# Unread transposes at two more places of a one-core trunk layer, and an earlier trace place for the sums of merged tokens

## Chip, cores and metric

The kernel runs on one core of one Trainium2 chip. The metric is device time in microseconds (us), the median of several runs; the kernel before was run three times. One further execution was taken with the profiler, and all rows below come from that one.

## What is computed

One layer of a decoder trunk with four parallel branches, on 256 tokens of width 2048, everything in fp32. The reference, cut to what matters here:

```python
xn = rms_norm(x, ln_g)
(a_q, a_k, a_v, a_g, c_b, c_c, c_h, c_g, s_q, s_k, s_v, s_g, m_q, m_g,
 i_q, i_k, i_w, r_a, r_c, r_s, r_m) = [xn @ w for w in cols]
y_a = moba_attention(a_q, a_k, a_v) * silu(a_g)
y_c = c_b * short_conv(c_c * c_h, conv_w, conv_b) * silu(c_g)
y_s = dsa_attention(s_q, s_k, s_v, i_q, i_k, i_w) * silu(s_g)   # indexer picks the keys
y_m = memory_attention(m_q, mk, mv) * silu(m_g)
merged = (sigmoid(r_a) * (y_a @ w_branch[0]) + sigmoid(r_c) * (y_c @ w_branch[1])
          + sigmoid(r_s) * (y_s @ w_branch[2]) + sigmoid(r_m) * (y_m @ w_branch[3]))
return rms_norm(x + merged @ w_out, final_g)
```

## The kernel before

**Products.** Every fp32 operand is split into a high and a low part of type fp32r, `hi` and `lo` (`split`, L108: a cast on ScalarE, L109, and a subtraction on VectorE, L110), and a product is three matmuls: hi by hi, hi by lo, lo by hi. Where the output is wanted transposed (queries, keys, gates), a block of 256 weight columns is the stationary operand and the 256 tokens are the moving one (`project_t`, `products_t`, L145 to L147): 2 column tiles x 16 chunks x 3 = 96 matmuls of 256 columns a block, four blocks for a section of width 1024. Otherwise the tokens are stationary and the weights move (`project`, `products`, L174 to L176), 512 columns at a time, or 256 in the last two blocks of the output projection. Some 512-column products are done by halves (`by_halves`, a Strassen-like scheme): weight quarters are subtracted from one another on VectorE (`held`, L265, L271, L275, L280) and meet sums of token parts (`sums_of`, L207; `x_sums` for the input, `m_sums` for the merged tokens).

**Weights' way.** SP loads a quarter of 1 MB into one of four slots with tag "raw" (L127 or L197); ScalarE and VectorE split it half by half into rings of four `hi` and `lo` tiles. The tiles `f` and `g` of `sums_of` take slots of the same tag "raw".

**Unread transposes.** `two_transposes` (L149) writes two transposes of the identity into a PSUM bank named `unused` with tag "s" (two banks, shared with the indexer's `lg`, the attention's `s` and the token transposes) that nothing reads. `project_t` calls it ahead of a block when `first` is true: at the first block of each section of queries and keys and at some others (nine pairs in all). `keep_in_program_order` pins each transpose behind the PE instruction traced before it; nothing pins later matmuls behind the transposes.

**Order.** The order of instructions on each engine is not written out by hand: a list scheduler with a timeline model picks, whenever an engine is free, the ready instruction that was traced first. So the place in the trace is a priority. The trace runs: memory branch, indexer (`indexer_parts`, L469; `indexer`, L489, with `lg` matmuls at L495 and L496 and a Relu at L498), sparse queries, keys and values (L637 to L639), sparse attention, the local attention branch, the convolution branch, and the output projection.

**The end.** `finish` (L625) runs, for each half `j` of a branch, the gate columns by halves and then `merge` (L524): the branch product with 512-column matmuls `w`, times the sigmoid, added to `merged`. For the last branch (L687) `parts_of` (L673) transposes merged columns behind each quarter and splits them into `mt`, and `merged_sums` (L684), called between the last gate columns and the last `merge`, allocates `m_sums`. `sums_of` on the first eight chunks of `mt` is traced behind it all, at L688: two additions of 1024 columns (L212), four of 512 (L214 to L217) and four splits. Then `blocks_of` (L704) yields the output projection: 512 columns as block 0, 1024 by halves (with `m_sums`), and blocks 3 and 4 of 256 columns each; every result is added to `x`, squared and scaled (L724 to L742).

Of the kernel before, what the change touches and what calls it, by code (L numbers as in the profile page):

```python
# [28 lines left out]
S_Q, S_K, S_V, S_G = 8 * W, 9 * W, 10 * W, 11 * W  # L29
# [9 lines left out]
FIRST = {}  # L39
# [11 lines left out]
def hybrid_kernel(ctx, tc, x, xT, mem, memT, ln_g, mem_ln_g, w_t, w_n, w_idx, conv_w, conv_b, w_mem_k, w_mem_v,  # L51
# [13 lines left out]
    def bank(name, tag):  # L65

        return banks.tile([P, NB], F32, name=name, tag=tag, bufs=1 if tag in ("pp", "yp") else 2)
# [40 lines left out]
    def split(hi, lo, src):  # L108
        nc.scalar.copy(out=hi, in_=src)  # L109
        nc.vector.tensor_sub(out=lo, in0=src, in1=hi.bitcast(F32))  # L110
# [10 lines left out]
    def split_weights(src, w):  # L121

        c = src.shape[2]
        per, half = 4 * NB // w, 2 * NB // w
        for k0 in range(0, src.shape[1], per):
            raw = raw_tile(w)[:, :, :c]
            nc.sync.dma_start(out=raw, in_=src[:, k0:k0 + per])  # L127
            for h0 in range(0, per, half):
                hi, lo = parts_tiles(w, c, STATIONARY if w == TB else 0)
                split(hi, lo, raw[:, h0:h0 + half])  # L130
                for k in range(half):
                    yield hi[:, k], lo[:, k], k0 + h0 + k
# [9 lines left out]
    def products_t(o, hi, lo, k, nk, act):  # L142

        a = act(k)
        nc.tensor.matmul(o, lhsT=hi, rhs=a[:, 0], start=(k == 0), stop=False)  # L145
        nc.tensor.matmul(o, lhsT=hi, rhs=a[:, 1], start=False, stop=False)  # L146
        nc.tensor.matmul(o, lhsT=lo, rhs=a[:, 0], start=False, stop=(k == nk - 1))  # L147

    def two_transposes():  # L149

        o = bank("unused", "s")
        for i in range(2):
            tc.keep_in_program_order(nc.tensor.transpose(o[:, i * P:(i + 1) * P], ident, ident))

    def project_t(src, act, first=False):

        if first:
            two_transposes()
        nk, c = src.shape[1:]
        tag = next(turn)  # L160
        acc = [bank("acc", tag)[:, :T] for _ in range(0, c, P)]
        for hi, lo, k in split_weights(src, TB):
            for j, c0 in enumerate(range(0, c, P)):
                c1 = min(c0 + P, c)
                products_t(acc[j][:c1 - c0], hi[:, c0:c1], lo[:, c0:c1], k, nk, act)
        return acc

    def copy_t(dst, acc, func=AF.Copy, rows=P):
        for j, a in enumerate(acc):
            nc.scalar.activation(out=dst[:, j], in_=a[:rows], func=func)  # L170
# [7 lines left out]
    def project(src, act, name, t_outer=False):  # L178

        nk, c = src.shape[1:]  # L180
        tag = next(turn)
        acc = [bank(name, tag)[:, :c] for t in range(2)]
        parts = split_weights(src, c)
        if t_outer:
            held = list(parts)
            steps = ((p, t) for t in range(2) for p in held)
        else:
            steps = ((p, t) for p in parts for t in range(2))
        for (hi, lo, k), t in steps:
            a = act(k)[:, :, t * P:(t + 1) * P]  # L190
            products(acc[t], a[:, 0], a[:, 1], hi, lo, k == 0, k == nk - 1)
        return acc
# [14 lines left out]
    def sums_of(act, sums):  # L207

        f = rawp.tile([P, 4 * NB], F32, name="f", tag="raw").rearrange("p (q k t) -> p q k t", q=2, t=T)
        g = rawp.tile([P, 4 * NB], F32, name="g", tag="raw").rearrange("p (s k t) -> p s k t", s=4, t=P)  # L210
        for i in range(2):
            nc.vector.tensor_add(f[:, i], act(4 * i, 4)[:, :, 0].bitcast(F32), act(4 * i, 4)[:, :, 1].bitcast(F32))  # L212
        a11, a21, a12, a22 = (f[:, i, :, t * P:(t + 1) * P] for i in range(2) for t in range(2))
        nc.vector.tensor_add(g[:, 0], a21, a22)  # L214
        nc.vector.tensor_sub(out=g[:, 1], in0=g[:, 0], in1=a11)
        nc.vector.tensor_sub(out=g[:, 2], in0=a11, in1=a21)
        nc.vector.tensor_sub(out=g[:, 3], in0=a12, in1=g[:, 1])  # L217
        for i in range(4):
            split(sums[:, i, :, 0], sums[:, i, :, 1], g[:, i])
# [105 lines left out]
    def nat_tile(name, tag="nat"):  # L325
        return big.tile([P, 2, W], F32, name=name, tag=tag)
# [26 lines left out]
    def to_heads(name, c0):  # L353

        dst = big.tile([P, 8, T], F32, name=name, tag=name)
        for b in range(4):
            copy_t(dst[:, 2 * b:2 * b + 2], project_t(w_t[FIRST[c0] + b], x_act, b == 0))
        return dst

    def to_values(c0, halved):  # L360
# [15 lines left out]
    def to_gate(c0, val):  # L376

        y = y_parts()
        for b in range(4):
            yt = yt_tile()  # L380
            copy_t(yt, project_t(w_t[FIRST[c0] + b], x_act, b == 0 and c0 == C_G), func=AF.Silu)
            gate_parts(y, yt, yt, val, 2 * b)
        return y
# [241 lines left out]
    def finish(b, y, halved=(True, True), after=None, last=None):  # L625

        for j in range(2):
            sig = gate_columns(b, j, halved[j])
            if j == 1 and last is not None:
                last()  # L630
            merge(b, j, sig, y, after)
# [3 lines left out]

    mask_s = indexer(*indexer_parts())
    q = to_heads("qt", S_Q)  # L637
    k = to_heads("kt", S_K)
    v = to_values(S_V, True)  # L639
    masked_attention(q, k, v, mask_s)  # L640
    finish(BR_S, to_gate(S_G, q))


    q = to_heads("qt", A_Q)
    k = to_heads("kt", A_K)
    v = to_values(A_V, True)
# [24 lines left out]
    mt = big.tile([P, KC, 2, T], F32R, name="mt", tag="xhl")  # L671
# [10 lines left out]
    m_sums = []  # L682

    def merged_sums():  # L684
        m_sums.append(big.tile([P, 4, 4, 2, P], F32R, name="m_sums", tag="m16b"))

    finish(BR_C, to_gate(C_G, cc), after=parts_of, last=merged_sums)  # L687
    sums_of(lambda k0, n: mt[:, k0:k0 + n], m_sums[0])  # L688


    xr = [big.tile([P, D], F32, name=f"xr{t}", tag=tag) for t, tag in ((0, "qt"), (1, "kt"))]
# [12 lines left out]
    def blocks_of():  # L704

        def block(n):
            c0, c = blocks[n]
            acc = project(w_out[c0 // NB][:, :, c0 % NB:c0 % NB + c], lambda k: mt[:, k], "o", t_outer=(n == last))
            return ((n, t, acc[t]) for t in range(2))

        yield from block(0)
        got = []
        nat = nat_tile("no")
        by_halves([w_out[1], w_out[2]], lambda k: mt[:, k], m_sums[0], nat,
                  lambda t, n, src, psum: got.append((1 + n, t, src)), ("y",))
        yield from got
        for n in range(3, last + 1):
            yield from block(n)

    for n, t, src in blocks_of():  # L720
        c0, c = blocks[n]
# [60 lines left out]
```

## Time and profile before

| what | value |
|---|---|
| runs of the kernel | 1362.73, 1363.07, 1364.81 us, median 1363.07 |
| the profiled execution, its own time | 1364.0 us |
| its span, first to last instruction | 1362.2 us |
| TensorE matmuls | 1352.2 us busy (99%), 8386 instructions |
| VectorE | 1007.4 us busy (74%) |
| ScalarE | 786.6 us busy (58%) |
| GpSimd | 11.2 us busy (1%) |
| bytes read from HBM | 265.88 MB, 197 GB/s over the span |

How to read it: an engine's busy time is the union of its records. Matmuls are pipelined, so their records overlap, and the distance between two starts says more than a duration. "PE" is TensorE's matmuls, "PEld" its weight loads, DVE VectorE, ACT ScalarE, SP the engine that issues the loads. Times of rows count from the start of the span.

### The profile page before, as it was taken

The numbers are of one execution on the slowest core, as the hardware profiler recorded it, in microseconds if no ns is written. First come the engines' busy times: TensorE is split into PE (matmuls) and PEld (weight loads), VectorE is DVE, ScalarE is ACT, GpSimd is POOL, SyncE is SP. The second block draws the span as 40 slices with busy tenths as digits, with TensorE's granted clock in tenths as the row PEclk, the third lists the DMA queues.
The fourth block names the chain that finished last, engine by engine and source line by source line (L and its number), as shares of the span: only waits on it lengthen the run. The fifth ranks groups of instructions, "written<-read, shape, count | busy, mean of one in ns | idle before, by whom it ended". The sixth has DMA issues, their size and how long they took to land.

```text
span 1362.2 us, 20606 instructions
## 1 busy us (share of the span) xinstructions
PE 1352.2 (99%) x8386; PEld 1214.2 (89%) x8386; DVE 1007.4 (74%) x1171; ACT 786.6 (58%) x1066; POOL 11.2 (1%) x26
## 2 busy tenths in 40 slices
PE   9999999999999999999999999999999999999997
PEld 9998998889999899888999899888888999888877
DVE  7687665784756878787545878887888758798786
ACT  7663665463445677646444678646455445656553
POOL 1000000000000000000000000000000000000000
PEclk9999999999999999999999999999999999999999
DMA  9864545655556454656555555566565556655752
GB/s 346 302 254 175 200 155 178 216 175 178 193 186 216 160 172 165 210 191 215 187 189 197 180 178 176 171 218 208 185 210 198 192 200 222 207 180 203 249 182 92
DMA packets 49966, 269.43 MB, mean 198 GB/s; under 512 B 6656, under 2 KB 17456, under 8 KB 19024
## 3 DMA queue, kind: packets, MB, share of 16 engines
q1 hardware_dynamic: 48960, 264.03, 56.1%
q0 software_dynamic: 624, 3.31, 0.7%
q8 instruction: 65, 1.06, 0.3%
q10 hardware_dynamic: 288, 0.79, 0.1%
q14 instruction: 29, 0.24, 0.0%
HBM read 265.88 MB, written 2.10 MB: 197 GB/s over the span
## 4 chain that ended last, share of the span: by engine, by line
PE 95%; DVE 2%; ACT 1%; DMA 1%; issue 1%; SPq 0%; POOLq 0%; POOL 0%; DVEq 0%; ACTq 0%
PE acc L145 12%; PE acc L146 11%; PE acc L147 11%; PE w L174 4%; PE w L176 4%; PE w L175 4%; PE u L174 4%; PE u L175 4%; PE u L176 4%; PE m L174 3%; PE m L175 3%; PE m L176 3%; PE y L175 2%; PE y L176 2%; PE x L175 2%; PE x L176 2%
## 5 line engine op out<-in xcount | busy, mean ns | idle before, releaser
L110 DVE TENSOR_TENSOR lo<-raw,hi 128x1024 fp32r<-128x1024 f32 (+1 forms) x472 | 561.5, 1199 | 296.9 <-ACT hi L109 293.1
L109 ACT CAST hi<-raw 128x1024 fp32r<-128x1024 f32 (+1 forms) x472 | 485.0, 1031 | 426.8 <-PE acc L146 149.0
L145 PE MATMUL acc<-x_hl,hi 128*128 128x256 f32 x1264 | 353.7, 280 | 0.0
L146 PE MATMUL acc<-x_hl,hi 128*128 128x256 f32 x1264 | 351.7, 278 | 0.0
L147 PE MATMUL acc<-x_hl,lo 128*128 128x256 f32 x1264 | 351.5, 278 | 0.0
L147 PEld LDWEIGHTS acc<-x_hl,lo 128*128 128x128 f32 x1264 | 237.2, 188 | 0.1
L145 PEld LDWEIGHTS acc<-x_hl,hi 128*128 128x128 f32 x1264 | 237.0, 187 | 0.1
L146 PEld LDWEIGHTS acc<-x_hl,hi 128*128 128x128 f32 x1264 | 237.0, 187 | 0.1
L110 DVE TENSOR_TENSOR lo<-held,hi 128x1024 fp32r<-128x1024 f32 x96 | 115.1, 1221 | 13.6 <-ACT hi L109 13.3
L109 ACT CAST hi<-held 128x1024 fp32r<-128x1024 f32 x96 | 100.2, 1054 | 13.4 <-PE u L176 4.6
L176 PE MATMUL w<-hi,y 128*128 128x512 f32 x256 | 99.7, 389 | 0.0
L175 PE MATMUL w<-lo,y 128*128 128x512 f32 x256 | 99.7, 389 | 0.0
L174 PE MATMUL w<-hi,y 128*128 128x512 f32 x256 | 98.6, 390 | 0.0
L176 PEld LDWEIGHTS w<-hi,y 128*128 128x128 f32 x256 | 48.1, 188 | 10.0
L175 PEld LDWEIGHTS w<-lo,y 128*128 128x128 f32 x256 | 48.1, 188 | 9.9
L174 PEld LDWEIGHTS w<-hi,y 128*128 128x128 f32 x256 | 48.0, 188 | 9.9
L174 PE MATMUL y<-hi,x_hl 128*128 128x512 f32 x132 | 51.7, 392 | 0.0
L176 PE MATMUL u<-hi,x_hl 128*128 128x512 f32 x132 | 51.6, 391 | 0.0
L175 PE MATMUL u<-lo,x_hl 128*128 128x512 f32 x132 | 51.4, 390 | 0.0
L174 PE MATMUL u<-hi,x_hl 128*128 128x512 f32 x132 | 51.4, 390 | 0.0
L176 PE MATMUL y<-hi,x_hl 128*128 128x512 f32 x132 | 51.4, 389 | 0.0
L175 PE MATMUL y<-lo,x_hl 128*128 128x512 f32 x132 | 51.4, 389 | 0.0
(317 smaller groups left out, 2363.6 us busy)
## 6 DMA issues: line engine op xcount, KB each, us to landing
raw<-in_w_n SPq DMA_DIRECT2D x96, 1024.0 KB, 4.9
raw<-in_w_t SPq DMA_DIRECT2D x76, 1024.0 KB, 5.0
raw<-in_w_branch SPq DMA_DIRECT2D x32, 1024.0 KB, 5.0
raw<-in_w_out SPq DMA_DIRECT2D x16, 1024.0 KB, 4.8
raw<-in_w_mem_k SPq DMA_DIRECT2D x8, 1024.0 KB, 5.5
raw<-in_w_mem_v SPq DMA_DIRECT2D x8, 1024.0 KB, 4.9
raw<-in_w_t SPq DMA_DIRECT2D x16, 256.0 KB, 5.8
raw<-in_memT SPq DMA_DIRECT2D x2, 1024.0 KB, 8.2
```

The costliest lines, as they stand in the source:

```text
L109: nc.scalar.copy(out=hi, in_=src)
L110: nc.vector.tensor_sub(out=lo, in0=src, in1=hi.bitcast(F32))
L145: nc.tensor.matmul(o, lhsT=hi, rhs=a[:, 0], start=(k == 0), stop=False)
L146: nc.tensor.matmul(o, lhsT=hi, rhs=a[:, 1], start=False, stop=False)
L147: nc.tensor.matmul(o, lhsT=lo, rhs=a[:, 0], start=False, stop=(k == nk - 1))
L174: nc.tensor.matmul(o, lhsT=ah, rhs=hi, start=start, stop=False, **kw)
L175: nc.tensor.matmul(o, lhsT=ah, rhs=lo, start=False, stop=False, **kw)
L176: nc.tensor.matmul(o, lhsT=al, rhs=hi, start=False, stop=stop, **kw)
```

## The change

Three edits. In `to_heads` the block with `b == 1` of the sparse queries gets a pair of unread transposes too. `sums_of` on the merged tokens is traced inside `merged_sums`, so ahead of the last branch's second `merge`, and no longer behind it. In `blocks_of` a pair of unread transposes is traced between the halved part and the last two blocks of 256 columns.

```diff
@@ -354,7 +354,7 @@
 
         dst = big.tile([P, 8, T], F32, name=name, tag=name)
         for b in range(4):
-            copy_t(dst[:, 2 * b:2 * b + 2], project_t(w_t[FIRST[c0] + b], x_act, b == 0))
+            copy_t(dst[:, 2 * b:2 * b + 2], project_t(w_t[FIRST[c0] + b], x_act, b == 0 or c0 == S_Q and b == 1))
         return dst
 
     def to_values(c0, halved):
@@ -683,9 +683,9 @@
 
     def merged_sums():
         m_sums.append(big.tile([P, 4, 4, 2, P], F32R, name="m_sums", tag="m16b"))
+        sums_of(lambda k0, n: mt[:, k0:k0 + n], m_sums[0])
 
     finish(BR_C, to_gate(C_G, cc), after=parts_of, last=merged_sums)
-    sums_of(lambda k0, n: mt[:, k0:k0 + n], m_sums[0])
 
 
     xr = [big.tile([P, D], F32, name=f"xr{t}", tag=tag) for t, tag in ((0, "qt"), (1, "kt"))]
@@ -714,6 +714,7 @@
         by_halves([w_out[1], w_out[2]], lambda k: mt[:, k], m_sums[0], nat,
                   lambda t, n, src, psum: got.append((1 + n, t, src)), ("y",))
         yield from got
+        two_transposes()
         for n in range(3, last + 1):
             yield from block(n)
 
```

## Rows read from the trace of the kernel before

**Rows 1.** The page: TensorE's granted clock by slice; the chain's shares by engine.
```profile
PEclk9999999999999999999999999999999999999999
...
PE 95%; DVE 2%; ACT 1%; DMA 1%; issue 1%; SPq 0%; POOLq 0%; POOL 0%; DVEq 0%; ACTq 0%
```

**Rows 2.** Timeline of PE, sparse queries and keys: start us, us, engine, line, operation.
```profile
355.63 0.28 PE L145 MATMUL acc<-x_hl,hi 128*128 128x256 f32 x1
...
389.20 0.38 PE L153 MATMUL unused<-ident 128*128 128x128 f32 x2
...
389.53 0.28 PE L146 MATMUL acc<-x_hl,hi 128*128 128x256 f32 x1
...
432.95 0.40 PE L174 MATMUL u<-hi,x_hl 128*128 128x512 f32 x1
```

**Rows 3.** Timeline of PE: first and last of the output's 256-column matmuls.
```profile
1331.96 0.28 PE L174 MATMUL o<-hi,mt 128*128 128x256 f32 x1
...
1354.46 0.28 PE L176 MATMUL o<-hi,mt 128*128 128x256 f32 x1
```

**Rows 4.** Timeline of PE at a pair behind 512-column products; the transposes' group.
```profile
656.50 0.38 PE L153 MATMUL unused<-ident 128*128 128x128 f32 x2
...
656.84 0.28 PE L146 MATMUL acc<-x_hl,hi 128*128 128x256 f32 x1
...
700.26 0.38 PE L153 MATMUL unused<-ident 128*128 128x128 f32 x2
...
L153 PE MATMUL unused<-ident x18: 270/271/273, 28.6 to 1095.9; 128*128 128x128 f32 x18
```

**Rows 5.** Timelines of PE and ACT where the sparse queries' second block begins.
```profile
354.61 0.60 PE L496 MATMUL lg<-it 128*128 128x256 f32 x2
354.86 0.47 PE L145 MATMUL acc<-x_hl,hi 128*128 128x256 f32 x1
...
355.29 0.38 PE L153 MATMUL unused<-ident 128*128 128x128 f32 x2
...
355.43 0.49 ACT L498 ACTIVATE sm<-lg 128x384 f32<-128x384 f32 x1
```

**Rows 6.** Timeline of PE at eight token transposes in the convolution branch.
```profile
1061.22 1.04 PE L350 MATMUL tp<-ident,uu 128*128 128x128 f32 x8
...
1062.22 0.28 PE L146 MATMUL acc<-x_hl,hi 128*128 128x256 f32 x1
...
1064.57 0.28 PE L145 MATMUL acc<-x_hl,hi 128*128 128x256 f32 x1
```

**Rows 7.** The sums' additions and splits, and their first reader (ns min/median/max, first to last start).
```profile
L212 DVE TENSOR_TENSOR f<-mt x2: 1219/1220/1220, 1248.1 to 1255.3; 128x1024 f32<-128x1024 f32 x2
...
L174 PEld LDWEIGHTS m<-hi,m_sums x5: 188/188/188, 1298.0 to 1308.7; 128*128 128x128 f32 x5
...
L110 DVE TENSOR_TENSOR m_sums<-g,m_sums x4: 682/686/689, 1252.9 to 1265.3; 128x512 fp32r<-128x512 f32 x4
```

**Rows 8.** Timelines of DVE and PE inside the last branch product.
```profile
1249.43 1.23 DVE L110 TENSOR_TENSOR lo<-raw,hi 128x1024 fp32r<-128x1024 f32 x1
...
1255.79 0.39 PE L175 MATMUL w<-lo,y 128*128 128x512 f32 x1
```

**Rows 9.** Chain, then timelines of DVE and PE, in the output's halved product.
```profile
1285.86 1.24 DVE lo L110
...
1287.12 7.54 DMA raw<-in_w_out
...
1294.68 2.29 DVE L275 TENSOR_TENSOR held<-raw 128x2048 f32<-128x2048 f32 x1 [2.15 <-DMA raw<-in_w_out]
...
1298.10 2.35 DVE L110 TENSOR_TENSOR lo<-held,hi 128x1024 fp32r<-128x1024 f32 x2
...
1298.63 0.39 PE L174 MATMUL x<-hi,mt 128*128 128x512 f32 x1
...
1306.02 0.39 PE L176 MATMUL x<-hi,mt 128*128 128x512 f32 x1
```

## The prediction

> **What bounds the kernel now.** I read the page first: 95% of the chain that ended last is TensorE's, nearly all of it matmuls, and its clock is granted at full speed, 2.4 GHz, in every slice [rows 1]. So the time is the number of matmuls times their pace, plus what little TensorE waits. Each edit then has to be priced at TensorE's queue; work on the other engines counts only where it makes TensorE late.
>
> Next I took the timeline of TensorE and, instead of durations (they overlap), the distance from one start to the next. The same 256-column matmul, at the same clock, runs at two paces. In the sparse queries' last three blocks it goes from 355.63 to 389.20, 285 steps by the 96 matmuls of a block: 33.57 / 285 = 0.1178 us a step. At 389.20 stand the two unread transposes of the sparse keys' first block, and from 389.53 to 432.95, where the 512-column product begins, 383 steps take 43.42 us: 0.1134 us [rows 2]. The slow pace costs 0.0044 us a matmul, and it does not mend itself over hundreds of them. What these rows show of the transposes is that the fast pace begins behind them.
>
> Third, the same reading of the output's last columns: 192 matmuls of 256 columns (two blocks, two token halves, 16 chunks, 3 products) from 1331.96 to 1354.46, 191 steps in 22.50 us, 0.1178 us: the slow pace again, with no transposes ahead [rows 3].
>
> **The change part by part.** *Price of a pair.* A pair starts at 389.20 and the second matmul behind it at 389.53 [rows 2]; without the pair one step, 0.11, would lie between, so it costs 0.33 - 0.11 = 0.22 us. Behind 512-column products it is 0.34 - 0.11 = 0.23 [rows 4]. A transpose's own record is 0.27 us, but that overlaps. No engine reads their bank. No DMA is added.
>
> *Output's last columns.* The pair is pinned behind the last matmul of the halved product, and the 256-column blocks are traced after it. The nearest rows are the pair at 656.50, which also stands between 512- and 256-column products: from the second matmul behind it, at 656.84, to the next pair, at 700.26, 383 steps take 43.42 us, 0.1134 [rows 4]. If it does so here, the 191 steps take 191 x 0.1134 = 21.66 instead of 22.50, a gain of 0.84, less the pair's 0.23: 0.61 us. Nothing covers these matmuls: what follows the last one, started at 1354.46 of a span of 1362.2, waits for it, so all of it is on the path. Bounds: +0.23 us (nothing restored) to -0.61; I take -0.61, the end whose row has the same neighbours.
>
> *Sparse queries.* Here the first block's own pair did not come ahead of its block: the second block begins at 354.86, 3 x 96 matmuls ahead of 389.20, and the pair stands at 355.29, two matmuls into it and just behind the last indexer matmuls; the pace behind it is slow [rows 2, 5]. The likely reason is their bank: it is one of two with tag "s", which the indexer's four logit tiles use too. The new pair is pinned behind the first block's last matmul and needs such a bank as well: either the one that the first pair gives back at once, or the one that the Relu of 355.43 reads, 0.49 us [rows 5]. So I place it a few matmuls behind 355.43. If it restores the fast pace, some 284 steps gain 0.0044 each, 1.25 us, less 0.22: 1.03. If not, it costs 0.22, and up to 0.5 more if TensorE stands at it until that Relu is through (everything on TensorE queues behind it then). The sparse keys' pair at 389.20 ends the stretch either way, so nothing later depends on it. For it: the pair at 389.20 came out of the slow pace. Against it: the pair at 355.29 stayed in it, and eight transposes at 1061.22, which stood in a fast stretch, left the 20 steps from 1062.22 to 1064.57 at 0.1175 [rows 6]. A transpose group does not always do it, above all when it falls in the middle of the stream beside other small matmuls. I take the gain, -1.03, as the likelier of two, and keep +0.7 as the other end.
>
> *Sums of the merged tokens.* No instruction is added; ten on VectorE and four on ScalarE, and two tiles of the weights' four-slot pool, get an earlier place in the trace, past the 4 weight loads of the last branch product on SP's queue, their splits, and the products' evictions. VectorE's part is 2 x 1.22 + 8 x 0.69 = 8.0 us by the two sizes [rows 7]; ScalarE's four casts run beside it. Yet the order of the trace is only a priority: already now the sums run inside that product, from 1248.1 on, and the last of the four is split at 1265.3, while its first reader, a weight load of the halved product, starts at 1298.0 [rows 7]. They have 32 us to spare, so finishing a few microseconds sooner is worth nothing by itself. They cannot start sooner by much: their second addition, at 1255.3, needs merged tokens that are transposed inside that product. What they push back is the weight splits. The split at 1249.43 ends at 1250.66, and TensorE first needs a low part of the next half tile at 1255.79 [rows 8], so the cover is about 5 us; the part of the sums that can be in one piece is what follows the second addition, 1.22 + 3 x 0.69 + 3 x 0.69 = 5.4 less overlaps. I cost it at 0. Bounds: -1.0 and +2.8, both below.
>
> **The sum.** -0.61 - 1.03 + 0 = -1.6 us against the profiled execution, which took 1364.0 us around its span of 1362.2: 1362.4. That execution lies 0.9 above the median of the runs shown, 1363.07, and on the median it is 1361.4.
>
> **The rivals.** *The sparse pair does not restore.* Price 0.22 to 0.7 instead of -1.03: 1361.4 + 1.3 to 1.8, about 1362.8. For it speaks 355.29, the nearest place of all; against it the distance from the indexer's matmuls.
>
> *Pairs change no pace.* Both only cost: 1363.07 + 0.22 + 0.23 = 1363.5. Against this speak the fast stretches behind two pairs [rows 2, 4]. The Trainium skill (TensorE: Matmul & The Clock Gate, section Back-to-back issue gap) gives a warm matmul one single gap, N / 2.4 + 2.5 ns, which is an estimate of 109 ns for 256 columns, and no second pace that a transpose could end; by that rule this rival would be the forecast. The trace disagrees with it: 113 and 118 ns at one and the same granted clock.
>
> *The stall in the last halved product goes as well.* From 1298.63 to 1306.02 there are 28 steps of 512 columns; at twice 0.1134 they would take 6.35 us and take 7.39: 1.04 us are lost. VectorE stands in a subtraction that waits for a weight quarter, whose load was asked for at 1287.12 and took 7.54 us, and the low parts that TensorE needs queue behind it, at 1298.10 [rows 9]. If the earlier sums give back two pool slots sooner and the plan puts those low parts ahead, the time is 1361.4 - 1.04 = 1360.4 or a little less. For it: the sums hold two of the four slots until 1265.3 at the latest [rows 7]. Against: that quarter's load takes the slot which the split of 1285.86 frees, 20 us later, when the sums are long over.
>
> *The sums starve the branch product (slower).* Place: the low parts of the half tile used at 1255.79. If all 8.0 us of VectorE's sums stand ahead of the split of 1249.43, its low part is 8.0 - 5.1 = 2.8 us late; if the two tiles also hold their slots from before the last weight quarters are asked for, a load falls in series, up to 7.54. That gives 1361.4 + 2.8 to 10.3; it ends over the bound of slower once more than 4.4 us are lost, and I put it at 1366. Against: the needed second addition cannot stand there.
>
> **How the numbers follow.** Chances: forecast 0.45, sparse pair in vain 0.22, pairs without effect 0.07, stall gone too 0.17, starved 0.09. The likeliest gives 1361.4. The range 1359.9 to 1363.9 takes in the first four, with half a microsecond for the scatter of a median (the three runs shown span 2.1 us), and leaves out the last. About 0.2%, 2.7 us, is what a measurement here can tell from no change: faster means below 1360.3, slower above 1365.8. The case of the vanished stall lies on that edge, so 0.12 of it and its like count as faster; of the starved case 0.08 counts as slower; the rest, 0.80, as the same.
>
> **What would show it.** Right: steps of 0.113 us from the new pair to the end of the sparse queries and through the output's last columns, whose 192 matmuls then take 21.7 us; the first wait in the last halved product where it was. Wrong: 0.118 behind either pair; the new sparse pair directly beside the old one with an idle TensorE until the Relu ends; a wait of TensorE for a low part inside the last branch product; the reader of the sums no longer late, or later.

## The result, and the profile after

The changed kernel takes 1375.71 us, median of four runs (1375.16 to 1377.05); the kernel before, beside it, 1363.08 (1362.73 to 1364.81). The ratio is 1.0088, 95% interval 1.0076 to 1.0100: 12.6 us slower, outside the predicted range. The profiled execution took 1377.05 us around a span of 1375.3.

The page first: TensorE's busy share, its granted clock, the chain's shares, and the groups of the last stage's `w` matmuls (columns: busy us, mean ns, idle before and its releaser).

```profile
PE   9999999999999999999999999999999999997997
...
PEclk9999999999999999999999999999999999998999
...
PE 95%; DVE 2%; ACT 1%; issue 1%; DMA 0%; POOLq 0%; POOL 0%; DVEq 0%; ACTq 0%
...
L174 PE MATMUL w<-hi,y 128*128 128x512 f32 x256 | 99.0, 393 | 8.3 <-ACT hi L109 8.3
```

The chain's shares are almost those of [rows 1] and would hide the loss; the slices and the group show it: one slice near the end in which TensorE is busy 7 tenths of the time and its clock is granted at 8 tenths, and 8.3 us idle in front of a `w` matmul, ended by a cast into `hi` on ScalarE.

To see which stage lost what, cut the span at the first matmul of each stage. Us, from the starts in the timelines of TensorE (pair: the sparse queries' first pair; keys' end: the first `u` of 512 columns; conv: the first `x` of either half of the convolution branch; output: the first `o` of 512 and of 256 columns).

| stretch | before | after |
|---|---|---|
| start to the queries' first pair | 354.10 | 356.19 |
| sparse queries and keys | 77.66 | 76.73 |
| to the convolution branch | 538.69 | 538.69 |
| convolution branch, first half | 172.20 | 172.92 |
| convolution branch, second half | 123.51 | 135.63 |
| output, 512 columns and by halves | 64.61 | 63.59 |
| output, last columns | 22.50 | 22.58 |
| behind the last matmul's start | 7.76 | 7.75 |

The first stretch differs by up to 3 us between the traces of these kernels, whose code is the same up to there. The loss is one row: 12.1 us in the second half of the convolution branch. Next the waits of that stretch, 1240 to 1262 us (engine, line, releaser: us, times, longest).

```profile
PEld w L174 <- ACT hi L109: 8.5, 1, 8.5
...
PEld pp L679 <- issue: 2.1, 2, 1.9
```

Then the timeline of TensorE at the places that the change touches: the sparse queries' and keys' pairs, the last branch product, and the end.

```profile
357.38 0.38 PE L153 MATMUL unused<-ident 128*128 128x128 f32 x2
...
359.96 0.38 PE L153 MATMUL unused<-ident 128*128 128x128 f32 x2
...
390.36 0.38 PE L153 MATMUL unused<-ident 128*128 128x128 f32 x2
...
1245.44 0.39 PE L176 MATMUL y<-hi,x_hl 128*128 128x512 f32 x1
1247.32 1.22 PE L679 MATMUL pp<-ident,merged 128*128 128x128 f32 x8 [1.49 <-DVE mt L110]
1256.80 1.22 PE L174 MATMUL w<-hi,y 128*128 128x512 f32 x2 [8.25 <-ACT hi L109]
...
1258.65 0.63 PE L176 MATMUL w<-hi,y 128*128 128x512 f32 x1
1259.08 0.63 PE L175 MATMUL w<-lo,y 128*128 128x512 f32 x1
...
1260.25 0.39 PE L175 MATMUL w<-lo,y 128*128 128x512 f32 x1
...
1344.94 0.36 PE L174 MATMUL o<-hi,mt 128*128 128x256 f32 x1
...
1367.52 0.28 PE L176 MATMUL o<-hi,mt 128*128 128x256 f32 x1
```

The pieces: 1.88 us from the last `y` to the eight `pp` transposes, where a step is 0.23 (1.65 lost); from the last of these, at 1248.27, to the first `w`, at 1256.80, 8.53 us in place of 0.11 (8.42 lost); and then seven steps of 512 columns that take 0.32 to 0.67 us, three of them 0.427, instead of 0.227 (3.46 us for 1.59: 1.87 lost). Together 11.9 of the 12.1 us. Most of the last piece is the clock. The table by stretch gives the granted clock (the column behind POOL) as 0.73 and 0.74 here, between stretches of 1.00; from 1250 to 1260 us it is 0.50, the lower level, 1.2 GHz, at which a step of 512 columns took 427 ns:

```profile
1250.00:1260.00 10.00, 3.17 (x7) 2.06 (x8) 9.63 (x13) 6.26 (x8) 0.00 (x0) 0.50 0.39 125
...
1243.00:1258.00 15.00, 5.26 (x23) 3.35 (x21) 12.79 (x19) 8.71 (x14) 0.00 (x0) 0.73 0.23 75
1258.00:1262.00 4.00, 3.96 (x14) 3.21 (x14) 3.41 (x4) 1.98 (x3) 0.00 (x0) 0.74 1.01 385
```

The first three of the seven steps, 0.59 to 0.67 us, are longer than the lower level alone makes them (1.86 us in place of 3 x 0.427 = 1.28). In them TensorE's weight load for a low part also waits for VectorE, by the same view of waits:

```profile
PEld w L175 <- DVE lo L110: 0.8, 1, 0.8
```

The Trainium skill (TensorE: Matmul & The Clock Gate, HAM oscillation — how this bites in real kernels) says that a long enough idle TensorE comes back throttled; by that rule the wait costs more than itself, and the trace agrees, with slow steps that lose 1.87 us on top of 8.42.

Why was the cast late? ScalarE's timeline, changed kernel:

```profile
1245.87 1.07 ACT L109 CAST mt<-pp 128x512 fp32r<-128x512 f32 x2 [1.13 <-PE y L176]
...
1247.98 1.18 ACT L109 CAST mt<-pp 128x512 fp32r<-128x512 f32 x2 [0.52 <-PE pp L679]
1250.86 0.62 ACT L109 CAST m_sums<-g 128x512 fp32r<-128x512 f32 x1 [1.70 <-DVE g L216]
1253.20 1.34 ACT L109 CAST m_sums<-g 128x512 fp32r<-128x512 f32 x2 [1.72 <-DVE g L214]
1255.18 0.62 ACT L109 CAST m_sums<-g 128x512 fp32r<-128x512 f32 x1 [0.64 <-DVE g L217]
1255.70 3.88 ACT L109 CAST hi<-raw 128x1024 fp32r<-128x1024 f32 x4
```

And the same engine in the kernel before:

```profile
1238.59 1.05 ACT L109 CAST hi<-raw 128x1024 fp32r<-128x1024 f32 x1 [0.54 <-PE u L176]
1241.55 1.05 ACT L109 CAST hi<-raw 128x1024 fp32r<-128x1024 f32 x1 [1.91 <-PE u L176]
...
1251.94 0.63 ACT L109 CAST m_sums<-g 128x512 fp32r<-128x512 f32 x1
```

ScalarE works through its instructions in the order that the scheduler gave it. Before, the weights' casts stood ahead of the first cast of the sums. After, four `hi` casts stand behind all four casts of the sums, and between those ScalarE waits three times (1.70, 1.72 and 0.64 us) for VectorE's additions. Were the weights there? Both quarters were asked for at 1237.55 and 1240.42 and took 5.1 us (median, from the DMA view of 1237 to 1241 us):

```profile
raw<-in_w_branch SPq DMA_DIRECT2D x2, 1024.0 KB, 5.1
```

So they lay in SBUF from about 1246 on, ten microseconds before the cast, which indeed shows no wait for a DMA. They had been asked for late, too: in the kernel before at 1222.95 and 1227.55, with slots that `f` and `g` hold here. But that is not what TensorE waits for. It waits for the order.

### The profile page after: what moved, and what is told of

It reads as the page before. It is cut to its first block, busy times and chain, and to the rows that moved or that the text cites. A ratio compares the mean times of both kernels' runs of the same rounds, so it can differ in the third digit from the quotient of the medians.

```text
span 1375.3 us, 20611 instructions
## 1 busy us (share of the span) xinstructions
PE 1355.8 (99%) x8390; PEld 1217.2 (89%) x8390; DVE 1007.9 (73%) x1171; ACT 787.2 (57%) x1066; POOL 11.2 (1%) x26
## 4 chain that ended last, share of the span: by engine, by line
PE 95%; DVE 2%; ACT 1%; issue 1%; DMA 0%; POOLq 0%; POOL 0%; DVEq 0%; ACTq 0%
PE acc L147 11%; PE acc L145 11%; PE acc L146 11%; PE w L174 4%; PE w L175 4%; PE w L176 4%; PE u L175 4%; PE u L174 4%; PE u L176 4%; PE m L174 3%; PE m L175 3%; PE m L176 3%; PE y L175 2%; PE y L176 2%; PE x L175 2%; PE x L176 2%
```

## The experiments

In every table of results the ratio is to the kernel before on the same chip, with its 95% interval. All these kernels compute the whole layer.

**1. Both pairs without the sums, and the sums without the pairs.** `e1_pairs_only` is the changed kernel with the call of `sums_of` back behind `finish`; `e2_sums_only` is

```diff
         m_sums.append(big.tile([P, 4, 4, 2, P], F32R, name="m_sums", tag="m16b"))
+        sums_of(lambda k0, n: mt[:, k0:k0 + n], m_sums[0])
     finish(BR_C, to_gate(C_G, cc), after=parts_of, last=merged_sums)
-    sums_of(lambda k0, n: mt[:, k0:k0 + n], m_sums[0])
```

> Both pairs of unread transposes, sums traced where they were. If the whole loss sits in the moved sums (my theory), this kernel is at or a little below the kernel before: the sparse queries' stretch behind the new pair runs at 0.1134 us a step, a gain of 266 x 0.0044 - 0.22 = 0.95 us, and the output's last columns stay at 0.1178 and pay the pair, 0.23 us; together -0.7 us, 1362.4 against 1363.1. Rival, the pairs disturb something else as well: 1365 or more. Rival, pairs change no pace: +0.45 us, 1363.5.

> Only the sums moved ahead of the last branch product, no new pair. If the loss is theirs alone, the time is that of the changed kernel plus the 0.7 us that the pairs give: about 1376.4, with TensorE idle for some 8.5 us ahead of the first matmul of the last branch product and a first cast of weights behind the four casts of the sums on ScalarE. Rival, the loss needs the pairs too: 1363 to 1366.

Pairs only: 1362.50 us, 0.9997 (0.9988 to 1.0006). Sums only: 1375.78 us, 1.0094 (1.0081 to 1.0108), with the same wait in the waits view:

```profile
PEld w L174 <- ACT hi L109: 8.5, 1, 8.5
```

The whole loss comes from the sums. Without the pairs the second half of the convolution branch takes 137.02 us, 13.5 more than before; here 14 steps are slow, not 7.

**2. Priority or room?** Moving the call does two things: the sums' operations get an earlier place, and `f` and `g` are handed their two slots of the weights' pool ahead of the last four quarters. `e3_sums_own_room` keeps the place and takes the room away, `e4_slots_early` keeps the room and takes the place away (with a first writer that waits for nothing, a memset of two columns that the addition overwrites).

```diff
# e3_sums_own_room, against e2_sums_only
+    def sums_of(act, sums, room=(rawp, "raw", rawp, "raw")):
+        f = room[0].tile([P, 4 * NB], F32, name="f", tag=room[1])...
+        g = room[2].tile([P, 4 * NB], F32, name="g", tag=room[3])...
+        sums_of(lambda k0, n: mt[:, k0:k0 + n], m_sums[0], (big, "qt", big, "kt"))
# e4_slots_early, against the kernel before, in merged_sums
+        m_sums.append(sums_room())
+        for v in m_sums[1]:
+            nc.gpsimd.memset(v[:, 0, 0, 0:2], 0.0)
```

> Sums traced early as in the changed kernel, no new pair, but their two work tiles lie in two other places that are free there (tags qt and kt) and take no slot of the weights' pool. Theory slots (the loss comes from two of four weight slots going to the sums ahead of the last branch's weights): no idle TensorE, 1362 to 1364. Rival priority (the early trace place alone puts the sums' casts ahead of the weights' casts on ScalarE): TensorE idle as before, 1373 to 1377.

> Sums traced late as in the kernel before, but each of their two work tiles gets a tiny first write (two columns set to zero on GpSimd) at the early place, so that the slots are taken early and held until the sums are done; no new pair. If late weight loads by themselves starve TensorE (slots alone): two weight loads asked for some 10 us later than before and the next two only when those are split, TensorE idle for 2 to 8 us, 1365 to 1371. If the loss needs the sums' casts ahead of the weights' casts in ScalarE's queue (priority and slots together): hardly any idle time, 1363 to 1365. Rival priority alone: 1363.

Own room: 1362.35 us, 0.9996 (0.9987 to 1.0005). Slots early: 1363.17 us, 1.0003 (0.9994 to 1.0012). TensorE has no idle time at the product's start in either. So neither the earlier place nor the lost slots costs anything alone.

**3. Both, with an early first writer.** `e8_early_claimed` is `e2_sums_only` plus the two memsets, so early place and shared slots, both.

```diff
+    def sums_of(act, sums, claim=False):
...
+        for v in (f, g) if claim else ():
+            nc.gpsimd.memset(v[:, 0, 0, 0:2], 0.0)
...
+        sums_of(lambda k0, n: mt[:, k0:k0 + n], m_sums[0], claim=True)
```

> Sums traced early, both in slots of the weights' pool, but each tile gets a first writer that waits for nothing: a GpSimd memset of two columns, which the addition behind it overwrites. Neither new pair. Theory (a slot is handed out in the order of the trace once its tile's first writer can be placed; with the additions as first writers the weight loads of the last branch product stand in the plan behind them): with the memset the slots are handed out at once, the loads of the weights are no longer planned behind the additions, the splits into hi go ahead of the sums' casts on ScalarE, and the 8.5 us of idle TensorE are gone: 1362 to 1364 us. Rival (the earlier priority of the sums' operations together with a pool that is short of two slots is enough, whoever writes first): the idle stays, at 1372 to 1377 us.

1362.43 us, 0.9999 (0.9990 to 1.0008), with no idle TensorE at the product's start: the rival is out. The three views that matter, ScalarE, then SP's queue, then GpSimd:

```profile
1240.52 2.00 ACT L109 CAST hi<-raw 128x1024 fp32r<-128x1024 f32 x2 [2.85 <-DMA raw<-in_w_branch]
...
1243.41 1.06 ACT L109 CAST hi<-raw 128x1024 fp32r<-128x1024 f32 x1 [0.36 <-DMA raw<-in_w_branch]
...
1252.68 0.62 ACT L109 CAST m_sums<-g 128x512 fp32r<-128x512 f32 x1 [0.47 <-DVE g L218]
```

```profile
1214.92 0.33 SPq L197 DMA_DIRECT2D raw<-in_w_n  x1
1235.30 13.68 SPq L127 DMA_DIRECT2D raw<-in_w_branch  x4
```

```profile
1222.61 0.10 POOL L212 MEMSET f<- 128x2 f32 x1 [77.36 <-DVE lo L110]
...
1227.21 0.10 POOL L212 MEMSET g<- 128x2 f32 x1 [1.49 <-DVE lo L110]
```

This is the cleanest run of the study. The first quarter is asked for at 1235.30, 20.4 us behind the load ahead of it; in the changed kernel the gap is just as long (1217.17 to 1237.55). The first two quarters are as late, and the time is that of before, because ScalarE casts them as they land. Late loads cost nothing here; the order in which ScalarE, VectorE and TensorE were told to work costs 12 us.

What remains of the explanation is the planner's reason, and that is inferred: no trace shows a plan. A tile's slot is handed out where its first writer is placed. With the additions as first writers, which need `mt`, the loads traced behind `f` and `g` stand in the plan behind the first addition (1247.81 in the trace after), with landing and casts later still; so the planner finds the sums and the `pp` transposes ready first and writes them ahead of the weights on three engines. With the memsets, which take their slots at 1222.61 and 1227.21, the loads are planned early. All six kernels with moved sums fit this.

**4. Between the two products.** `e7_between_products` traces the sums after the third quarter of the merge, so two of the last four weight quarters stand ahead of `f` and `g`, two behind.

```diff
+    def parts_and_sums(n, merged):
+        parts_of(n, merged)
+        if n == 2:
+            sums_of(lambda k0, n: mt[:, k0:k0 + n], m_sums[0])
-    finish(BR_C, to_gate(C_G, cc), after=parts_of, last=merged_sums)
+    finish(BR_C, to_gate(C_G, cc), after=parts_and_sums, last=merged_sums)
```

> Sums traced between the two products of the last merge, so two of the last four weight quarters are traced ahead of the tiles f and g and two behind them; slots of the weights' pool as before; neither new pair. Theory (the loss is the weights traced behind f and g that are planned late): half of the weights come ahead, TensorE has the first product's 128 matmuls (29 us) as a cover for the others: no idle of over 1 us ahead of the first product, 1362 to 1365 us. Rival (what costs is the sums' work itself, standing in that stretch on ScalarE and VectorE ahead of anything traced later): the second product's splits are late in turn, and the time is 1368 to 1376.

1369.82 us, 1.0049 (1.0035 to 1.0063). My number missed, the rival's held. TensorE:

```profile
1254.50 0.39 PE L176 MATMUL w<-hi,y 128*128 128x512 f32 x1
1257.06 0.41 PE L679 MATMUL pp<-ident,merged 128*128 128x128 f32 x2 [2.17 <-DVE merged L540]
1258.77 1.54 PE L679 MATMUL pp<-ident,merged 128*128 128x128 f32 x6 [1.31 <-DVE merged L540]
1259.97 1.20 PE L174 MATMUL w<-hi,y 128*128 128x512 f32 x2
```

The order is that of the changed kernel, at the second product: the `pp` transposes stand ahead of it, and its weights are cast behind three of the sums' four casts (two `hi` casts at 1256.27). But here the casts are not what TensorE waits for: they are done before its first `w` at 1259.97, which shows no wait. It waits ahead of the transposes, 2.17 and 1.31 us, for VectorE's additions into `merged` (L540), and between VectorE's evictions stand operations of the sums:

```profile
1255.03 0.68 DVE L215 TENSOR_TENSOR g<-g,f 128x512 f32<-128x512 f32 x1
1255.63 0.68 DVE L539 TENSOR_TENSOR sig<-w,sig 128x512 f32<-128x512 f32 x1
...
1256.83 0.69 DVE L110 TENSOR_TENSOR m_sums<-g,m_sums 128x512 fp32r<-128x512 f32 x1
1257.43 0.69 DVE L217 TENSOR_TENSOR g<-f,g 128x512 f32<-128x512 f32 x1
1258.03 0.69 DVE L540 TENSOR_TENSOR merged<-merged,sig 128x512 f32<-128x512 f32 x1
```

Behind these waits the second product begins at the lower clock, 0.50 from 1258 to 1264 us. My cover was wrong too: I gave the first product 128 matmuls, 29 us; it has 48 (two token halves, 8 chunks, 3 products), 10.9 us. The rival's number was right, and so in part was its reason: the sums' work stands in VectorE's way here, though run 3 shows that their early place alone does not put it there.

**5. The output's last columns.** Behind the end pair the pace stays slow: in the changed kernel 191 steps from 1344.94 to 1367.52 take 22.58 us, 118.2 ns each with the pair's long first step, against 117.8 in [rows 3]. Is it where the operands lie? `e5_place` has the sparse pair alone and puts the `hi` and `lo` tiles of the 256-column blocks 0 bytes into their buffers in place of 64; `e6_place_and_pair` has the end pair too; `p32`, `p128` and `p192` are `e5_place` with other offsets, there alone.

```diff
-        parts = split_weights(src, c)
+        parts = split_weights(src, c, 0)          # 32, 128 or 192 if c == TB
```

> The sparse queries' pair alone; sums where they were; no pair at the output's last columns, but there the hi and lo tiles of the 256-column blocks begin at the start of their ring buffers, as those of the 512-column blocks do, no longer 64 bytes in. Theory (the slow pace of the output's last columns hangs on where their operands lie, which transposes cannot change): 0.113 us a step there in place of 0.118, 0.85 us less; with the sparse pair's 0.8 to 0.9 some 1361.0 us. Rival (it hangs on what TensorE did before, and this edit leaves that as it is): the pace there stays 0.118, and the time is 1361.8 to 1362.0, the sparse pair's gain alone.

> As the run without the end pair, with the pair ahead of the output's last columns too, and the hi and lo tiles there at the start of their buffers. If place alone sets the pace: 0.113 us a step, and the pair only costs its 0.23 us, 1361.2. If pair and place are both needed: 0.113 here and 0.118 in the run without the pair, 1361.2 here against 1361.9 there. If neither has to do with it: 0.118 in both, and 1362.1 here.

> The sparse queries' pair alone; the hi and lo tiles of the output's 256-column blocks begin 32 bytes into their buffers (64 in the kernel before, where a step took 117.8 ns; at 0 it took 120.0 ns). Theory (the distance of the operands' places sets the pace, and the right one has not been hit): one of 32, 128 and 192 bytes gives 113 to 114 ns. Rival (what is missing is the order of the roles: here the weights are the moving operand): 117.8 or 120 at every place.

> As the run at 32 bytes, with 128 bytes. Theory of the places: 113 to 114 ns at one of the three. Rival: 117.8 or 120 ns at every place.

> As the run at 32 bytes, with 192 bytes. Theory of the places: 113 to 114 ns at one of the three. Rival: 117.8 or 120 ns at every place.

| bytes | 0 | 0, with the end pair | 32 | 64 (before) | 128 | 192 |
|---|---|---|---|---|---|---|
| ns a step, 191 steps | 120.0 | 120.4 | 116.7 | 117.8 | 120.0 | 117.8 |
| time, us | 1363.29 | 1362.87 | 1362.88 | 1362.89 or 1362.73 | 1362.42 | 1362.62 |

First and last step at 32 bytes:

```profile
1331.06 0.28 PE L174 MATMUL o<-hi,mt 128*128 128x256 f32 x1
...
1353.35 0.28 PE L176 MATMUL o<-hi,mt 128*128 128x256 f32 x1
```

Neither theory as written: the place does set the pace, by up to 3.3 ns, and 0 equals 128 as 64 equals 192; but none of the five places reaches 113.4. The pair only costs: 0.14 us ahead of the stretch (63.61 against 63.47) and 0.08 in it. 0.2 us could be had at 32 bytes; in the time of the program none of this can be told apart (`e5_place` 1.0005, 0.9996 to 1.0013; `e6_place_and_pair` 1.0001, 0.9992 to 1.0010; the other three have one run each).

**6. The whole change, mended.** `e9_whole_claimed` is the changed kernel plus the two memsets.

> The whole change, all three edits, and with it the GpSimd memset of two columns as first writer of each of the sums' two tiles. If the loss lies only in the plan's late place for the weights behind f and g, which the memset takes away, the time is that of both pairs with the sums where they were, 1362 to 1363 us (the changed kernel takes 1375.7), with no idle time at the last branch product's start. If the pairs and the earlier sums together did something that neither does alone, it stays over 1366.

1362.62 us, 0.9999 (0.9990 to 1.0008), no idle time at the product's start. Nothing else is in the 12 us.

**7. Where the sparse pair's gain goes.** In all eight kernels so far with the added pair the sparse stretch is 0.93 us shorter, as in the table of stretches above, and in every one the first half of the convolution branch is 0.6 to 1.3 us longer: 173.33 against 172.20 in `e1_pairs_only`. There one weight load, asked for at about 1000 us, takes longer. From `e1_pairs_only`, the DMA view at that load (last column: us to landing), and VectorE's waits of 1003 to 1014 us:

```profile
raw<-in_w_n SPq DMA_DIRECT2D x1, 1024.0 KB, 6.4
```

```profile
DVE held L265 <- DMA raw<-in_w_n: 1.3, 1, 1.3
```

The kernel before has 4.9 there, and no such wait. (The expectations below count the load from the end of its issue, 0.33 us later than this view does.) Two things differ: the program has two transposes more ahead of the load, and everything behind them runs 0.9 us earlier. Four runs to tell them apart: `f1_one_pair_later` moves the queries' only pair 16 matmuls further into the second block, `f2_pair_doubled` writes it twice at one place, `g1_pair_swapped` adds the new pair and drops the sparse keys' own, `g2_keys_pair_added` adds a pair in the keys, where the pace is fast already. `f3_one_pair_place32` is `f1` with the 32 bytes of run 5.

```diff
-            copy_t(..., project_t(w_t[FIRST[c0] + b], x_act, b == 0))
# g1_pair_swapped
+            copy_t(..., project_t(w_t[FIRST[c0] + b], x_act, b == 0 and c0 != S_K or c0 == S_Q and b == 1))
# g2_keys_pair_added
+            copy_t(..., project_t(w_t[FIRST[c0] + b], x_act, b == 0 or c0 == S_K and b == 1))
# f1_one_pair_later: two_transposes() ahead of chunk 3 of block 1 instead of ahead of block 0
# f2_pair_doubled: two_transposes() twice ahead of block 0
```

> The sparse queries' only pair moved: not in the first block's name any more (where it stood two matmuls into the second block and changed no pace) but pinned behind the third weight chunk of the second block, so some 18 matmuls into it. The program has as many TensorE instructions as the kernel before, and nothing else is moved. If a pair standing there starts the fast pace, as the second pair 22 matmuls into that block did: 0.1134 us a step from there, some 268 steps, 1.2 us less in that stretch. For the weight load asked for at about 1000 us, which took 5.6 to 6.2 us in every program with the added pair and 4.4 to 4.7 in every one without: if the two added instructions are its cause (they shift what comes behind them in TensorE's stream), it takes 4.4 to 4.7 here, no stall follows, and the time is about 1361.5. If the 0.9 us by which the stages behind come earlier are the cause, it takes 5.6 to 6.2, a stall of 0.5 to 0.9 follows, and the time is about 1362.2.

> The kernel before, with the sparse queries' own pair written twice (four transposes at one place, two matmuls into the second block). Two TensorE instructions are added, and the pace there is expected to stay at 0.1178 us, since one pair at that place changed nothing. If added instructions make the load of about 1000 us late, it takes 5.6 to 6.2 us, a stall of 0.5 to 0.9 us follows near 1010, and the time is 1363.2 to 1364. If the earlier time is the cause: 4.4 to 4.7, no stall, and the price of the pair alone, 0.2 us more than before.

> As the run with the one pair moved, and the output's 256-column blocks' hi and lo tiles 32 bytes into their buffers, where a step took 116.7 ns in place of 117.8: 0.2 us less than that run, some 1361.3 us if no stall follows at 1010, 1362.0 if one does.

> The sparse queries' added pair kept, and the sparse keys' own pair (at 389.20 in the kernel before) taken out: as many TensorE instructions as in the kernel before from the sparse keys on. If the fast pace that the added pair starts holds without a further pair, 0.1134 us a step through the queries' last blocks and the keys alike, 0.9 us gained there and the keys' pair (0.22) saved. For the weight load asked for at about 1000 us: if two added instructions in TensorE's stream make it late, it takes 4.4 to 4.7 us here and no stall follows near 1010: 1361.3 to 1361.8. If the 0.9 us by which everything behind comes earlier make it late, it takes 5.6 to 6.2, a stall of 0.5 to 0.9 follows, and the time is 1362.1 to 1362.5.

> The kernel before, with a second pair in the sparse keys (ahead of their second block), where the pace is the fast one already: two added TensorE instructions and no earlier time, 0.2 us later if anything. If the added instructions make the load of about 1000 us late: 5.6 to 6.2 us, and a stall of 0.5 to 0.9 near 1010. If the earlier time is the cause: 4.4 to 4.7 and no stall. The pace behind the added pair is expected to stay at 0.1134.

| kernel | transposes added | sparse queries and keys, us | that load, us to landing | conv branch, first half, us | time, us | ratio |
|---|---|---|---|---|---|---|
| before | | 77.66 | 4.9 | 172.20 | 1363.40 beside f1 and f2, 1362.92 beside g1 and g2 | |
| f1_one_pair_later | 0 | slow pace behind its pair | 5.0 | 172.19 | 1362.35 | 0.9994 (0.9986 to 1.0003) |
| f2_pair_doubled | 2 | 76.73 | 6.2 | 173.1 | 1362.30 | 0.9993 (0.9984 to 1.0002) |
| g1_pair_swapped | 0 | 76.49 | 4.9 | 172.20 | 1361.84 | 0.9990 (0.9981 to 0.9999) |
| g2_keys_pair_added | 2 | 77.90 | 6.0 | 173.00 | 1363.71 | 1.0008 (0.9999 to 1.0017) |

`g1_pair_swapped` and `g2_keys_pair_added` tell the two apart. Earlier time without added transposes (the first): the load is on time. Added transposes without earlier time (the second): the load is late and VectorE waits for it. All traces of this study agree: 5.9 to 6.5 us in the ten kernels with two transposes added ahead of the load, 4.7 to 5.0 in the nine without. The views of `g1`, then of `g2`:

```profile
raw<-in_w_n SPq DMA_DIRECT2D x1, 1024.0 KB, 4.9
```

```profile
raw<-in_w_n SPq DMA_DIRECT2D x1, 1024.0 KB, 6.0
```

```profile
DVE held L265 <- DMA raw<-in_w_n: 0.9, 1, 0.9
```

What two transposes do to a load 600 us later is seen only in part. A load ends with sixteen 4-byte packets, as many as the core has DMA engines. In the kernel before all of this load's closing packets stand 3.87 to 4.57 us behind the ask; in `e1_pairs_only` fifteen come by 4.67 and the last at 6.02, in `g2_keys_pair_added` by 4.46 and at 5.58. One closing packet of sixteen is late. In each of these traces a packet of 16 KB on the instruction queue, some 0.95 us long, falls into the load's last part. The Trainium skill (Runtime: NRT & Kernel Launch, Instruction fetch mechanics) says that an engine's instructions are fetched by DMA in blocks of 16 KiB, mostly hidden; two instructions more would shift which of them begins a block. That such a fetch occupies the engine that then closes late is my reading, and it isn't shown: the traces don't say which engine carried it, and the packet is there in the kernels with the load on time too. It begins 4.1 to 4.5 us behind the ask in these and 2.8 to 4.3 in the late ones, so its place alone doesn't tell them apart.

Misses in this group: `f1` did not start the fast pace behind its pair. Its timeline shows more than that:

```profile
354.93 0.28 PE L145 MATMUL acc<-x_hl,hi 128*128 128x256 f32 x1
...
356.63 0.38 PE L153 MATMUL unused<-ident 128*128 128x128 f32 x2
...
356.97 0.28 PE L146 MATMUL acc<-x_hl,hi 128*128 128x256 f32 x1
...
388.66 0.38 PE L153 MATMUL unused<-ident 128*128 128x128 f32 x2
```

With no pair two matmuls into the block, its start runs fast: 15 steps from 354.93 to 356.63, 113 ns each. Behind the pair it is 117.8 ns up to the keys' pair. So a pair can end the fast pace as well as begin it, and the slow pace of the kernel before may come from the queries' own pair at 355.29. A kernel without any pair there was not run. And `f2`'s second pair was placed 20 matmuls behind the first, where the bank came free, which is where the changed kernel has it, so `f2` is the sparse edit by itself. `f3_one_pair_place32`, built on a pair that failed, took 1362.29 us, 0.9994 (0.9985 to 1.0002), with 116.7 ns at the end.

`g1_pair_swapped` is the one version here whose interval lies below the kernel before, and only just.

## Why the prediction was wrong

**The sums** are the failed step: I wrote "I cost it at 0", with bounds -1.0 and +2.8, and they cost 12.1 to 13.5 us. The step rested on "They cannot start sooner by much: their second addition, at 1255.3, needs merged tokens that are transposed inside that product." That was the order of one plan, read as a dependence. The tokens were there: in the trace after, the `pp` transposes run at 1247.32, ahead of the product, and the second addition at 1250.74. "The order of the trace is only a priority" was true of the operations and false of the slots: I had seen that two tiles of the four-slot pool move past four loads, and put only the work into the sum.

**The starved rival**, at 0.09, was the right side and the right neighbourhood, with wrong place and price. I put it at the low parts of 1255.79 and at 2.8 to 10.3 us, a subtraction or a load in the way. It is the first high parts, behind ScalarE's casts of the sums; and to the idle 8.42 us come 1.87 in slow steps, mostly of the low clock, which no term of mine had, and 1.65 ahead of the transposes. My objection to it was the sentence quoted above, so one error set both the term and the chance.

**The sparse queries** came true at their place: forecast 1.03 us, measured 0.93 (77.66 to 76.73). The pair stands 22 matmuls into the second block, 2.58 us behind the first, not directly behind the Relu, so some 265 steps gained, not 284. No TensorE idle time was added. The gain was then lost to a cause that my list lacked: "the sparse keys' pair at 389.20 ends the stretch either way, so nothing later depends on it" is wrong by 0.6 to 1.3 us, through the late load at 1000 us. The rival "does not restore" is out. But the reading behind both, that the pair at 355.29 stood in a slow pace and failed to end it, rested on the two matmuls ahead of it. `f1` without that pair begins the block fast, and there a pair ends the fast pace; what a pair does depends on more than my rows showed, so the right number here had some luck in it.

**The output's last columns**: forecast 0.61 us gained, measured a loss of 0.22, the pair's price as I had it and nothing for it. The step that failed was taking the pair at 656.50 as the nearest row because its neighbours have the same sizes [rows 4]. The operands' roles are exchanged there: weights stationary at 656.50, moving here. The same pair, the same sizes, another stream. That the roles decide it fits all five places tried, but no run exchanged them alone.

**Pairs change no pace**, the rule of a single gap, is refuted again by the sparse pair: 117.9 ns in the 19 steps ahead of it, 113.4 behind. At the output's end it would have been right about the pair, though not about a single gap: 116.7 to 120.4 ns, by place.

**The stall in the last halved product** isn't in the trace after: the stretch takes 63.59 us against 64.61, as that rival said. Its reason, the earlier sums, isn't needed: `e1_pairs_only`, with the sums where they were, takes 63.61 too, and in all ten kernels with added transposes it is 63.5 to 63.6, with the load of [rows 9] on time (4.9 to 5.6 us). Of the nine without, `before`, `e7_between_products` and `g1_pair_swapped` have the stall (64.4 to 64.6, that load 7.4 to 7.5 us), two have 63.7 (6.7 us), and four, among them `e3_sums_own_room` and `e8_early_claimed`, 63.5. So the added transposes, which go with a late load at 1000 us, go with a load on time here. Why is not shown, with one trace of each kernel. Nor is it shown whether the stall explains the 0.9 us by which the profiled execution of before lay above its median.

The remaining numbers fit: 0.93 gained, 0.72 lost in the convolution branch, 12.12 in its second half, 0.08 at the end, 1.02 gained where before's execution had its stall, 2.09 in the first stretch by execution: 13.05, the difference of the two spans, 1375.27 and 1362.22.

## What to carry to other kernels

Where a scheduler picks by trace order, a move in the trace also moves a tile's claim on its pool: count every load traced behind a claimed tile, and ask when that tile's first writer can be placed; a trivial early writer (here a memset of two columns) kept the plan in order. Never read a dependence out of where one plan happened to put an instruction. And a small gain far ahead should be followed to the end of the program: compare the stages one by one, since two transposes added at 360 us cost up to 1.3 us at 1010.

## What was not expected of the hardware

- A weight load's time goes with the number of TensorE instructions ahead of it: asked for at about 1000 us, it took 4.7 to 5.0 us in the nine programs without added transposes and 5.9 to 6.5 in the ten with two added ahead of it, one closing packet of sixteen 0.9 to 1.5 us behind the others.
- The same wait of 8.5 us was followed by 7 slow steps in the changed kernel (1.87 us lost) and by 14 in `e2_sums_only` (3.29 us lost); 1.42 us more, and their losses, 12.1 and 13.5 us, differ by about as much. The granted clock was 0.50 from 1250 to 1260 us in the one and from 1250 to 1263 in the other.
- 256-column matmuls at one granted clock run at 113.4, 116.7, 117.8 and 120.0 ns a step. In the stream with stationary weights a pair of transposes can switch 117.8 to 113.4 (at 389.20 in the kernel before, at 359.96 in the changed one), 113 to 117.8 (at 356.63 in `f1_one_pair_later`) or nothing (the added pair of `g2_keys_pair_added`, in a fast stretch); what decides is not known. With moving weights the place of the operand changes the pace, and the pair did not.
